# Two gate tiles to a bank, and the first chunk of the seven-product groups read at another distance

## The chip, the cores and the metric

One Trainium2 chip, one of its cores. The metric is the time of the whole launch in device microseconds (us), as the median of several runs.

## The reference

A two-layer decoder trunk in float32 on 256 tokens of width 2048. Layer 0 is a recurrent block (RG-LRU) and a SwiGLU feed-forward; layer 1 is sliding-window attention over one shared K/V and a second SwiGLU. What matters here:

```
def rg_lru(xb, w_rg, b_rg, w_ig, b_ig, lam):
    r = sigmoid(block_diag_linear(xb, w_rg, b_rg))      # 8 blocks of 256 x 256
    i = sigmoid(block_diag_linear(xb, w_ig, b_ig))
    log_a = -LRU_C * r * softplus(-lam)
    a = exp(log_a)
    u = sqrt(-expm1(2.0 * log_a)) * (i * xb)
    ...                                                 # h = scan of a*h + u
def recurrent_block(...):
    y_branch, x_branch = split(rms_norm(x, g) @ w_in)
    hs = rg_lru(conv(x_branch), ...)
    return x + (hs * gelu(y_branch)) @ w_out
def swiglu_ffn(x, g, w_in, w_out):
    gate, up = split(rms_norm(x, g) @ w_in)
    return x + (silu(gate) * up) @ w_out
```

## The kernel before

**Tiles and chunks.** Activations lie transposed, 128 features by 256 tokens to a tile. Each weight matrix is streamed once, in chunks of 128 x 1024 (512 KB: two blocks of 128 input features by 512 outputs). A chunk is a "job": `load` starts its DMA four jobs ahead into one of four `raw` buffers, `split` cuts it three jobs ahead into `hi` (ACT, L374) and `lo = raw - hi` (DVE, L375), one of four `hi` and four `lo` buffers, and the job's matmuls read them. A product of two float32 numbers is three matmuls, hi*hi, hi*lo and lo*hi. So an ordinary chunk is 24 matmuls of 128 x 128 by 256 columns (L422), and PE frees a `hi` buffer when the last matmul that reads it is done.

**The recurrent block.** `ORDER` sets the jobs: x groups (8 chunks each, then convolution), gate jobs g0 to g7 (one chunk of 24 matmuls each, L969) and y groups (8 chunks, then GELU), in the order x0 x1 x2 g0 x3 g1 y0 g2 g3 y1 g4 g5 y2 g6 g7 y3, and after them the projection `lru_out`. A gate job makes four 128 x 256 results, two for r and two for i. Before, each has its own PSUM bank of 512 columns, half of it unused, and ACT reads each with a Sigmoid. After every second gate job the task `recur` is started: Exp and Tanh on ACT, then products on DVE, Sqrt on ACT, a product and a scan (L1013) on DVE. The y task ends in `split_act`: a Copy on ACT and a subtraction on DVE give the tile z that `lru_out` multiplies with.

**Activation tables.** Sigmoid, Sqrt, and the pair Exp/Tanh each need another table on ACT. Where two neighbours on ACT's queue need different ones, an ACT_TABLE_LOAD stands between them.

**Order.** The kernel is recorded as one program; background tasks (convolution, `recur`, GELU, norms) are stepped between matmuls. A scheduling framework then orders each engine's queue by its own estimates of when operands are ready and puts in the waits. Dependences on PSUM go by whole banks. PSUM has eight banks; `bank()` hands out the one that has been free longest, `bank4()` a set of four.

**The seven-product groups.** In the input projection of each feed-forward, 9 of the 22 groups are `fast_group`s (`FAST`): in seven of their eight chunks (`PAIRS`; chunk 3 is plain) a 2 x 2 block product is done with seven products of 3 matmuls, 21 in place of 24 (L631). Three products read the chunk's `hi`/`lo`, four read mixed weights mh and ml that `mix` makes on DVE and ACT three jobs ahead. These are tiles of the pool `s0` to `s36`. A tile spacer of 64 bytes lies between `s0`-`s6` (the near ones) and `s7`-`s36` (the far ones); the mixed inputs lie in far tiles. "Distance" in this text is how far apart the two SBUF operands of a matmul lie, in bytes modulo 512: with mixed weights in near tiles it is 448, with far ones 0. A job's third entry chooses: 1 takes near tiles, 2 far ones.

```
            todo = ((5, part(a, 0), old(1)), (3, part(b, 0), old(3)), (2, com(3), old(2)),
                    (7, com(0), new(0)), (6, com(2), new(1)), (4, com(1), new(2)), (1, part(b, 1), new(3)))
            if c in self.EVEN:
                todo = todo[3:] + todo[:3]
```

Before chunk 4 the previous product group's results are transposed on PE (`flush`, L827). Elsewhere `LEVEL` names jobs whose `lo` lies so that eight of their matmuls have distance 0.

Of the kernel before, what the change touches and what calls it, by code (L numbers as in the profile page):

```python
# [14 lines left out]
AF = mybir.ActivationFunctionType  # L15
ALU = mybir.AluOpType

P = 128
D = 2048
T = 256  # L20
# [28 lines left out]
class Trunk:  # L49
# [16 lines left out]
    PLAIN = 4  # L66
    FAST = tuple(range(4, 21, 2))
    PAIRS = (0, 1, 2, 4, 5, 6, 7)
    EVEN = (0, 4)
    OWED = 9000.0  # L70
    BUSY = 780.0
    WORK = 37
# [551 lines left out]
    def fast_group(self, src, xn, mx, g, done, final):  # L624

        nc = self.nc
        st = {"begun": set()}

        def put(h, x, w, n=1):
            b = h // 2  # L630
            nc.tensor.matmul(st["ps"][b][:, h % 2 * T:(h % 2 + n) * T], x, w, start=b not in st["begun"], stop=True,  # L631
                             skip_group_check=True)
            st["begun"].add(b)

        def plain(c, hi, lo):

            x2 = [self.need(xn[2 * c + kt]) for kt in range(2)]
            wide = []
            for kt in range(2):
                for i in range(2):  # L640
                    xh, xl = (x2[kt][:, q * T + i * P:q * T + i * P + P] for q in range(2))
                    for x, w in ((xh, hi), (xl, hi), (xh, lo)):
                        wide.append((2 - 2 * i, x, w[:, kt * 2 * T:kt * 2 * T + 2 * T]))
            todo = [(h + e, x, w[:, e * T:e * T + T]) for h, x, w in wide for e in range(2)]
            for k, t in enumerate(todo):
                if k == len(todo) // 2:
                    self.half_tick()
                put(*t)

        def fast(c, hi, lo):  # L650

            a, b = (self.need(xn[2 * c + kt]) for kt in range(2))
            m = self.need(mx[c])
            mh, ml = self.mixed.pop(self.at)
            part = lambda s, q: (s[:, q * P:q * P + P], s[:, T + q * P:T + q * P + P])
            com = lambda q: (m[:, q * P:q * P + P], m[:, 2 * T + q * P:2 * T + q * P + P])
            old = lambda q: (hi[:, q * T:q * T + T], lo[:, q * T:q * T + T])
            new = lambda q: (mh[:, q * T:q * T + T], ml[:, q * T:q * T + T])
# [4 lines that stand above are left out]
            for n, (h, (xh, xl), (wh, wl)) in enumerate(todo):  # L663
                if n == 4:
                    self.half_tick()
                put(h, xh, wh)
                put(h, xl, wh)
                put(h, xh, wl)
            self.free(mh)
            self.free(ml)  # L670
            if final:
                self.free(m)

        for c in range(8):
            def mm(hi, lo, c=c):
                if c == 0:
                    st["ps"] = self.bank4()
                if c == self.EVEN[1]:
                    self.flush()
                (fast if c in self.PAIRS else plain)(c, hi, lo)  # L680
                if c == 7:
                    done(st["ps"])
            self.jobs.append((src(c), mm, (c in self.PAIRS) + (c in self.EVEN)))

# [225 lines left out]
    def lru(self, gains, rn):  # L910
        self.late = []
        nc, par = self.nc, self.par
# [45 lines left out]
        def gates(n):  # L958

            def mm(hi, lo):  # L960
                x2 = [self.need(xb[2 * n + kt]) for kt in range(2)]
                ps = [self.bank() for _ in range(4)]
                for j in range(4):
                    if j == 2:
                        self.half_tick()
                    for kt in range(2):
                        c = ((j // 2) * 2 + kt) * 256 + (j % 2) * P
                        for high, q in ((1, 0), (1, T), (0, 0)):
                            nc.tensor.matmul(ps[j][:, 0:T], (hi if high else lo)[:, c:c + P], x2[kt][:, q:q + T],  # L969
                                             start=kt == 0 and high > q, stop=kt == 1 and not high)  # L970
                v = []
                for j in range(4):
                    o = self.slot(F32)
                    col = (C_BR, C_BI)[j // 2] + 2 * n + j % 2
                    self.a(o[:, 0:T], ps[j][:, 0:T], AF.Sigmoid, bias=par[:, col:col + 1])
                    self.free_bank(ps[j])
                    v.append(o)
                for kt in range(2):
                    self.free(x2[kt])
                both.extend([(2 * n, v[0], v[2]), (2 * n + 1, v[1], v[3])])  # L980
                if n % 2:
                    self.spawn(recur(list(both)))
                    both.clear()
            self.jobs.append((self.d["gate"][n], mm, False))
# [3 lines left out]
        def recur(v):  # L988

            A = lambda s: s[:, 0:T]  # L990
            B = lambda s: s[:, T:2 * T]
            for k, r, i in v:
                self.a(B(r), A(r), AF.Exp, scale=self.cc[:, k:k + 1])
                self.a(A(r), A(r), AF.Tanh, scale=self.cc[:, 16 + k:17 + k])
                yield
                self.tt(B(i), A(i), A(xf[k]), ALU.mult)
                yield
            for k, r, i in v:
                self.stt(A(r), B(r), 1.0, A(r), ALU.add, ALU.mult)
                yield  # L1000
            for k, r, i in v:
                self.a(B(r), A(r), AF.Identity, bias=1.0)
                self.stt(A(r), A(r), 2.0, A(r), ALU.add, ALU.mult)
                yield
            for k, r, i in v:
                self.a(A(r), A(r), AF.Sqrt, scale=-1.0)
            yield
            for k, r, i in v:
                self.tt(A(i), A(r), B(i), ALU.mult)
                yield  # L1010
                self.dve += 350
                h = xf[k]
                self.nc.vector.tensor_tensor_scan(A(h), B(r), A(i), 0.0, ALU.mult, ALU.add)  # L1013
                hs[k].ap = h
                hs[k].ready = True
                self.free(r)
                self.free(i)
                yield
# [465 lines left out]
```

## Time and profile before

| | |
|---|---|
| median of 3 runs | 1943.24 us (1942.21 to 1943.66) |
| the profiled execution | 1942.83 us |
| its span, first to last instruction | 1941.0 us |
| PE / DVE / ACT busy | 1935.5 / 1521.2 / 1118.3 us |
| granted clock of PE over the span | 1.000 |

The recurrent block with its projection takes the first 320 us or so, the first feed-forward runs to about 1020 us, K/V and attention to 1190 us, and the second feed-forward takes the rest. Times in the rows are us from the span's start. A matmul's own duration is longer than its place in the stream: matmuls overlap, so what one costs is the time from its start to the next one's.

### The profile page before, as it was taken

To read this page: it belongs to the slowest core of one execution; us is meant where nothing else is said; L and a number is where in the kernel's file an instruction comes from. 1 tells how busy PE (TensorE), PEld (TensorE's weight loads), DVE (VectorE), ACT (ScalarE), POOL (GpSimd) and SP (SyncE) were. 2 spreads that over 40 slices of the span, in tenths; PEclk is the share of its full clock that TensorE was granted. 3 is DMA by queue.
4 is the path that set the end of the run, shared out by engine and by line. 5 is a ranking of instruction groups with operands and counts; after the bars stand their busy time and mean duration, and the time that the engine had idled before them with its cause. 6 is when DMAs were issued, how large, how long until landed. Compare 5 with 4: busy or idle time off the path is not lost.

```text
span 1941.0 us, 40252 instructions
## 1 busy us (share of the span) xinstructions
PE 1935.5 (100%) x16604; PEld 1908.5 (98%) x16604; DVE 1521.2 (78%) x2356; ACT 1118.3 (58%) x1583; POOL 4.4 (0%) x12
## 2 busy tenths in 40 slices
PE   9999999999999999999999999999999999999999
PEld 9999999999999999999998789999999999999999
DVE  7989868999989988545667886799999989944443
ACT  7798746556555557434556765555555555743332
POOL 0000000000000000000000000000000000000000
PEclk9999999999999999999999999999999999999999
DMA  8555666566665557565555435665656666666663
GB/s 282 185 184 186 218 217 196 188 206 208 206 204 199 193 200 255 187 198 193 195 186 193 144 120 198 204 199 193 206 199 205 211 206 202 237 198 206 206 202 125
DMA packets 107576, 385.36 MB, mean 199 GB/s; under 512 B 12032, under 2 KB 14208, under 8 KB 107392
## 3 DMA queue, kind: packets, MB, share of 16 engines
q1 hardware_dynamic: 106848, 381.86, 59.2%
q8 instruction: 130, 2.13, 0.4%
q0 software_dynamic: 256, 0.52, 0.1%
q14 instruction: 54, 0.44, 0.1%
q10 hardware_dynamic: 288, 0.40, 0.1%
HBM read 375.92 MB, written 6.29 MB: 197 GB/s over the span
## 4 chain that ended last, share of the span: by engine, by line
PE 97%; DVE 1%; ACT 1%; issue 0%; DVEq 0%; ACTq 0%
PE b L422 68%; PE b L631 18%; PE b L1369 5%; PE b L603 2%; PE b L1206 1%; DVE lo L375 1%; PE b L1163 1%; ACT s L137 1%; PE b L827 0%; DVE s L150 0%; PE b L1282 0%; PE b L1255 0%; ACT hi L374 0%; ACT L137 0%; PE b L1413 0%
## 5 line engine op out<-in xcount | busy, mean ns | idle before, releaser
L422 PE MATMUL b<-s,hi 128*128 128x256 f32 x7936 | 1018.6, 276 | 0.8 <-ACT s L137 0.7
L422 PEld LDWEIGHTS b<-s,hi 128*128 128x128 f32 x7936 | 962.1, 188 | 1.8 <-ACT s L137 1.2
L375 DVE TENSOR_TENSOR lo<-raw,hi 128x1024 fp32r<-128x1024 f32 (+1 forms) x579 | 702.0, 1219 | 332.5 <-ACT hi L374 323.6
L374 ACT ACTIVATE hi<-raw 128x1024 fp32r<-128x1024 f32 (+1 forms) x579 | 607.7, 1056 | 483.0 <-PE b L422 416.2
L422 PE MATMUL b<-s,lo 128*128 128x256 f32 x3968 | 586.2, 277 | 0.0
L422 PEld LDWEIGHTS b<-s,lo 128*128 128x128 f32 x3968 | 512.8, 188 | 0.0
L389 ACT ACTIVATE s<-s 128x1024 fp32r<-128x1024 f32 x126 | 131.6, 1057 | 169.6 <-DVE s L388 169.6
L631 PE MATMUL b<-s,s 128*128 128x256 f32 x1512 | 195.9, 279 | 0.0
L631 PEld LDWEIGHTS b<-s,s 128*128 128x128 f32 x1512 | 183.0, 189 | 0.0
L631 PE MATMUL b<-hi,s 128*128 128x256 f32 x1044 | 178.0, 277 | 0.0
L391 DVE TENSOR_TENSOR s<-s,s 128x1024 fp32r<-128x1024 f32 x126 | 153.5, 1219 | 5.9 <-ACT s L389 5.9
L631 PEld LDWEIGHTS b<-hi,s 128*128 128x128 f32 x1044 | 152.4, 188 | 0.0
L631 PE MATMUL b<-lo,s 128*128 128x256 f32 x522 | 132.5, 276 | 0.0
L390 DVE TENSOR_TENSOR lo<-raw,hi 128x768 fp32r<-128x768 f32 x126 | 118.4, 950 | 0.0
L137 ACT ACTIVATE s<-s 128x512 fp32r<-128x512 f32 (+3 forms) x179 | 87.7, 521 | 52.5 <-DVE s L146 31.1
L386 DVE TENSOR_TENSOR s<-raw 128x512 f32<-128x512 f32 x126 | 86.4, 686 | 39.4 <-DMA raw<-in_ffn_in 39.1
L385 ACT ACTIVATE hi<-raw 128x768 fp32r<-128x768 f32 x126 | 102.8, 834 | 12.3 <-ACT s L389 6.4
L631 PEld LDWEIGHTS b<-lo,s 128*128 128x128 f32 x522 | 92.7, 188 | 0.0
L1369 PE MATMUL b<-hi,s 128*128 128x512 f32 x256 | 81.5, 400 | 0.0
L146 DVE TENSOR_TENSOR s<-s,s 128x512 fp32r<-128x512 f32 (+2 forms) x145 | 75.8, 549 | 2.0 <-ACT s L137 2.0
L137 ACT ACTIVATE s<-s,par 128x256 fp32r<-128x256 f32 (+1 forms) x96 | 46.6, 513 | 26.0 <-DVE s L146 25.3
L146 DVE TENSOR_TENSOR s<-b,s 128x512 f32<-128x512 f32 (+2 forms) x106 | 55.5, 554 | 3.8 <-ACT s L137 2.5
(119 smaller groups left out, 1132.4 us busy)
## 6 DMA issues: line engine op xcount, KB each, us to landing
raw<-in_ffn_in SPq DMA_DIRECT2D x352, 512.0 KB, 3.4
raw<-in_ffn_out SPq DMA_DIRECT2D x176, 512.0 KB, 4.2
raw<-in_lru_in SPq DMA_DIRECT2D x63, 512.0 KB, 4.0
raw<-in_lru_out SPq DMA_DIRECT2D x32, 512.0 KB, 3.5
raw<-in_w_q SPq DMA_DIRECT2D x32, 512.0 KB, 3.3
raw<-in_w_o SPq DMA_DIRECT2D x32, 512.0 KB, 3.3
raw<-in_gate SPq DMA_DIRECT2D x8, 512.0 KB, 3.9
away<-s SPq DMA_DIRECT2D x8, 512.0 KB, 3.8
```

Of the source, the lines that this page charges most:

```text
L137: self.nc.scalar.activation(out, in_, func, **kw)
L146: self.nc.vector.tensor_tensor(out, a, b, op)
L374: self.nc.scalar.activation(hi[:, q], raw[:, q], AF.Copy)
L375: self.nc.vector.tensor_tensor(lo[:, q], raw[:, q], hi[:, q].bitcast(F32), ALU.subtract)
L385: act(hi[:, q], raw[:, q], AF.Copy)
L386: tt(two(d[:, 0:2 * T]), two(raw[:, T:3 * T]), raw[:, 0:T].unsqueeze(1).to_broadcast([P, 2, T]), ALU.subtract)
L389: act(mh[:, :], d[:, :], AF.Copy)
L390: tt(lo[:, q], raw[:, q], hi[:, q].bitcast(F32), ALU.subtract)
L391: self.mark = tt(ml[:, :], d[:, :], mh[:, :].bitcast(F32), ALU.subtract)
L422: self.nc.tensor.matmul(ps[f][:, 0:c1 - c0], w, x2[k][:, c0:c1], start=f not in begun, stop=last and all(q[1] != f for q in todo[n + 1:]))
L631: nc.tensor.matmul(st["ps"][b][:, h % 2 * T:(h % 2 + n) * T], x, w, start=b not in st["begun"], stop=True, skip_group_check=True)
L1369: nc.tensor.matmul(st[g][b][:, :], x, q, start=c + kt == 0 and x is xh and q is wh, stop=c == 7 and kt == 1 and q is wl)
```

## The change

A gate job takes two banks in place of four and writes two results to each. The accumulation is opened by the first matmul of the bank alone, and a bank is given back after its second Sigmoid. In the product groups `EVEN` keeps chunk 4 alone: chunk 0 now takes near tiles for its mixed weights and does its `hi`/`lo` products first, as chunks 1, 2, 5, 6 and 7 do. The place of the transposes (`TURN`) stays before chunk 4.

```diff
-    EVEN = (0, 4)
+    EVEN = (4,)
+    TURN = 4
...
-                if c == self.EVEN[1]:
+                if c == self.TURN:
                     self.flush()
                 (fast if c in self.PAIRS else plain)(c, hi, lo)
...
             def mm(hi, lo):
                 x2 = [self.need(xb[2 * n + kt]) for kt in range(2)]
-                ps = [self.bank() for _ in range(4)]
+                ps = [self.bank() for _ in range(2)]
+                cut = [ps[j // 2][:, j % 2 * T:j % 2 * T + T] for j in range(4)]
                 for j in range(4):
                     if j == 2:
                         self.half_tick()
                     for kt in range(2):
                         c = ((j // 2) * 2 + kt) * 256 + (j % 2) * P
                         for high, q in ((1, 0), (1, T), (0, 0)):
-                            nc.tensor.matmul(ps[j][:, 0:T], (hi if high else lo)[:, c:c + P], x2[kt][:, q:q + T],
-                                             start=kt == 0 and high > q, stop=kt == 1 and not high)
+                            nc.tensor.matmul(cut[j], (hi if high else lo)[:, c:c + P], x2[kt][:, q:q + T],
+                                             start=j % 2 + kt == 0 and high > q, stop=True, skip_group_check=True)
...
-                    self.a(o[:, 0:T], ps[j][:, 0:T], AF.Sigmoid, bias=par[:, col:col + 1])
-                    self.free_bank(ps[j])
+                    self.a(o[:, 0:T], cut[j], AF.Sigmoid, bias=par[:, col:col + 1])
+                    if j % 2:
+                        self.free_bank(ps[j // 2])
```

The change moves instructions on every engine of the recurrent block, since other banks and other times of readiness go into the framework's order. In the whole program ACT has 25 table loads before and 31 now; the six more all stand between g3 and the end of y3. The first place is ACT's queue at the gate jobs g2 and g3. Tiles `s_1679` and `s_1682` are g2's, `s_1714` and `s_1717` g3's; `<-b` rows are Sigmoids, `cc` rows Exp and Tanh, and `hi_80`, `hi_81`, `hi_78` splits of later chunks. Before, from the first Sigmoid of g3 on:

```order
L137 ACTIVATE s_1714<-b_143,par 128x256
L137 ACTIVATE s_1714<-b_144,par 128x256
L137 ACTIVATE s_1717<-b_145,par 128x256
L137 ACTIVATE s_1717<-b_142,par 128x256
L137 ACT_TABLE_LOAD
L137 ACTIVATE s_1679<-s_1679,cc 128x256 x4
L374 ACTIVATE hi_81<-raw_77 128x1024
L137 ACTIVATE s_1714<-s_1714,cc 128x256 x4
L374 ACTIVATE hi_78<-raw_74 128x1024
```

The same place now:

```order
L138 ACTIVATE s_1714<-b_145,par 128x256 x2
L138 ACT_TABLE_LOAD
L138 ACTIVATE s_1679<-s_1679,cc 128x256
L138 ACT_TABLE_LOAD
L138 ACTIVATE s_1717<-b_142,par 128x256 x2
L138 ACTIVATE s_1679<-s_1679,cc 128x256
L138 ACT_TABLE_LOAD
L138 ACTIVATE s_1679<-s_1679,cc 128x256
L375 ACTIVATE hi_81<-raw_77 128x1024
L138 ACTIVATE s_1679<-s_1679,cc 128x256
L138 ACTIVATE s_1714<-s_1714,cc 128x256 x4
L375 ACTIVATE hi_78<-raw_74 128x1024
```

Two Sigmoids of g3 have moved behind an Exp, so there are two more table loads ahead of the split of `hi_81`, and one Exp or Tanh fewer. At g4 and g5, and again at g6 and g7, a Sqrt task is cut in the same way, with two more loads each. The second place is ACT's queue after y3 has left PE. Tiles `s_2371` and `s_2414` carry the Sqrt of g6 and g7, `s_2692`, `s_2883` and `s_2886` the Tanh of y3, and `s_2898` is the z tile of `lru_out`'s seventh chunk. Before:

```order
L137 ACT_TABLE_LOAD
L137 ACTIVATE s_2371<-s_2371 128x256
L374 ACTIVATE hi_80<-raw_76 128x1024
L137 ACTIVATE s_2371<-s_2371 128x256
L137 ACTIVATE s_2414<-s_2414 128x256 x2
L137 ACTIVATE s_2692<-h_90 128x256
L137 ACTIVATE s_2883<-h_91 128x256
L374 ACTIVATE hi_81<-raw_77 128x1024
L137 ACTIVATE s_2883<-h_92 128x256
L137 ACTIVATE s_2886<-s_2692 128x256
L374 ACTIVATE hi_78<-raw_74 128x1024
L137 ACT_TABLE_LOAD
```

Now, from the split that comes next after that of `hi_78`:

```order
L375 ACTIVATE hi_79<-raw_75 128x1024
L138 ACT_TABLE_LOAD
L138 ACTIVATE s_2371<-s_2371 128x256 x2
L138 ACTIVATE s_2414<-s_2414 128x256 x2
L375 ACTIVATE hi_80<-raw_76 128x1024
L375 ACTIVATE hi_81<-raw_77 128x1024
L375 ACTIVATE hi_78<-raw_74 128x1024
L138 ACT_TABLE_LOAD
L138 ACTIVATE s_2692<-s_2692 128x256
L138 ACTIVATE s_2883<-s_2883 128x256
L375 ACTIVATE hi_79<-raw_75 128x1024
```

The Sqrt stood ahead of the splits of the second half of `lru_out`'s first group; now it stands behind four more splits (those of `hi_80`, `hi_81`, `hi_78`, `hi_79`), and the Tanh behind a further three. On PE, 11 matmuls of the next group now stand ahead of the first that reads `s_2898`. The third place is PE's queue at chunk 0 of a product group, with `s9_5114` and `s16_5115` the mixed weights and `s15_3902` and `s27_3922` the inputs. Before:

```order
L631 MATMUL b3_144<-s9_5114,s27_3922 128x256 x2
L631 MATMUL b3_144<-s16_5115,s27_3922 128x256
...
L631 MATMUL b0_141<-s9_5114,s15_3902 128x256 x2
L631 MATMUL b0_141<-s16_5115,s15_3902 128x256
L631 MATMUL b2_143<-hi0_78,s15_3902 128x256 x2
L631 MATMUL b2_143<-lo0_82,s15_3902 128x256
```

Now:

```order
L632 MATMUL b2_143<-hi0_78,s15_3902 128x256 x2
L632 MATMUL b2_143<-lo0_82,s15_3902 128x256
...
L632 MATMUL b3_144<-s0_5114,s27_3922 128x256 x2
L632 MATMUL b3_144<-s5_5115,s27_3922 128x256
L632 MATMUL b3_144<-s0_5114,s27_3922 128x256 x2
L632 MATMUL b3_144<-s5_5115,s27_3922 128x256
```

The nine matmuls on `hi` and `lo` come first, and the twelve on mixed weights read `s0` and `s5`, near tiles, where they read `s9` and `s16`, far ones. So it is in all 18 product groups.

## Rows read from the trace of the kernel before

**Rows 1.** The page: span, and busy time of each engine.

```profile
span 1941.0 us, 40252 instructions
PE 1935.5 (100%) x16604; PEld 1908.5 (98%) x16604; DVE 1521.2 (78%) x2356; ACT 1118.3 (58%) x1583; POOL 4.4 (0%) x12
```

**Rows 2.** Two stretches: length, busy us of each engine, clock, DMA share, GB/s.

```profile
127.00:227.00 100.00, 99.03 (x858) 98.06 (x857) 89.92 (x168) 88.43 (x163) 0.00 (x0) 1.00 0.57 185
382.00:753.00 371.00, 371.00 (x3262) 371.00 (x3261) 339.71 (x471) 218.67 (x264) 0.00 (x0) 1.00 0.61 207
```

**Rows 3.** Timeline of PE where y2 begins: start, us, what, count.

```profile
155.28 0.28 PE L969 MATMUL b<-s,lo 128*128 128x256 f32 x1
155.69 1.59 PE L422 MATMUL b<-s,hi 128*128 128x256 f32 x8
157.11 1.12 PE L422 MATMUL b<-s,lo 128*128 128x256 f32 x8
```

**Rows 4.** Timeline of PE at g7 and where y3 begins.

```profile
180.68 0.28 PE L969 MATMUL b<-s,lo 128*128 128x256 f32 x1
181.11 0.48 PE L969 MATMUL b<-s,hi 128*128 128x256 f32 x2 [0.15 <-DVE h L146]
...
183.90 0.28 PE L969 MATMUL b<-s,lo 128*128 128x256 f32 x1
184.87 1.59 PE L422 MATMUL b<-s,hi 128*128 128x256 f32 x8 [0.69 <-ACT s L137]
```

**Rows 5.** The critical chain in `w_o`: start, us, what; the same matmuls twice.

```profile
1133.34 8.18 PE b L603 x72
...
1166.29 8.48 PE b L603 x72
```

**Rows 6.** Timeline of PE at a product group's chunks 0 and 1.

```profile
423.75 1.60 PE L631 MATMUL b<-s,s 128*128 128x256 f32 x12
...
426.22 0.39 PE L631 MATMUL b<-hi,s 128*128 128x256 f32 x2
...
427.24 1.52 PE L631 MATMUL b<-s,s 128*128 128x256 f32 x12
428.60 0.39 PE L631 MATMUL b<-hi,s 128*128 128x256 f32 x2
```

**Rows 7.** Timeline of ACT after the Sigmoids of g3.

```profile
130.80 1.28 ACT L137 ACT_TABLE_LOAD   x1
132.09 1.71 ACT L137 ACTIVATE s<-s,cc 128x256 f32<-128x256 f32 x4
133.71 1.05 ACT L374 ACTIVATE hi<-raw 128x1024 fp32r<-128x1024 f32 x1
```

**Rows 8.** Timeline of ACT: splits of later chunks of y1's and y3's surroundings.

```profile
165.15 1.05 ACT L374 ACTIVATE hi<-raw 128x1024 fp32r<-128x1024 f32 x1
...
188.15 1.10 ACT L374 ACTIVATE hi<-raw 128x1024 fp32r<-128x1024 f32 x1
```

**Rows 9.** Timeline of PE: the first matmuls that read three splits.

```profile
136.35 1.41 PE L422 MATMUL b<-s,hi 128*128 128x256 f32 x11
...
169.91 0.84 PE L422 MATMUL b<-s,hi 128*128 128x256 f32 x6
...
193.65 1.07 PE L422 MATMUL b<-s,hi 128*128 128x256 f32 x8
```

**Rows 10.** Timeline of PE in `lru_out`: chunks two and seven of its first group.

```profile
211.84 1.86 PE L422 MATMUL b<-s,hi 128*128 128x256 f32 x15
...
223.68 1.98 PE L422 MATMUL b<-s,hi 128*128 128x256 f32 x16
```

**Rows 11.** Timeline of DVE after y3: a scan, a split, two elementwise steps.

```profile
215.20 0.68 DVE L1013 TENSOR_TENSOR_SCAN s<-s,s 128x256 f32<-128x256 f32 x1
...
218.46 1.22 DVE L375 TENSOR_TENSOR lo<-raw,hi 128x1024 fp32r<-128x1024 f32 x1
219.60 0.75 DVE L146 TENSOR_TENSOR s<-s,s 128x256 fp32r<-128x256 f32 x2
```

## The prediction

> **What bounds the kernel now.** I read the page first [rows 1]: PE is busy for 1935.5 of a span of 1941.0 us at the full granted clock, DVE for 1521.2, ACT for 1118.3. So an edit pays only through PE's stream: by a shorter step from one matmul's start to the next, or by a wait that goes or comes. Then the two stretches that the change touches [rows 2]. Where the product groups are, 382 to 753 us, PE is busy for all of 371.00 us and ACT for only 218.67. In the recurrent block, 127 to 227 us, PE is busy for 99.03 of 100.00 and ACT for 88.43: ACT has 11.6 us to spare there, and less than that in any one place. The little idle time of PE is read in its timeline around the gates [rows 3, 4].
>
> Two more readings carry sizes. The first is what a wait leaves behind. In the projection after attention the same 72 matmuls take 8.18 us, and 8.48 us after a wait [rows 5]: 0.1136 and 0.1178 us each. The slow step of 0.0042 us per matmul more stays until a chunk comes in which eight matmuls have distance 0; how many matmuls lie between is counted in the program. The second is distance: of two neighbouring product chunks with the same 21 matmuls, chunk 0 (mixed weights at distance 0) takes 426.22 - 423.75 = 2.47 us and chunk 1 (at 448) 428.60 - 426.22 = 2.38 [rows 6].
>
> **The product groups.** Nothing is added or removed there: twelve matmuls of chunk 0 go from distance 0 to 448, and nine on the chunk's own weights go first. Chunk 0 becomes a chunk 1: 0.09 us less, in 18 groups: 18 x 0.09 = 1.6 us. The near tiles are shared with the chunks before and after, so the mixing for chunk 1 may have to wait a little longer for them; ACT's 152 us to spare in 371 [rows 2] cover that, and chunks 1, 2 and 5 to 7 already follow each other so without a wait. From below: no gain, if the step depends on something else than distance; from above 2 us. I take -1.6.
>
> Beside this stands a rule of the Trainium skill (SBUF — State Buffer, section on who interferes with whom): PE reads moving data and weights through two independent ports and waits for nobody there. By it distance could not matter and this term would be 0. The rows say otherwise: the twelve mixed matmuls alone are busy for 1.60 us in chunk 0 and 1.52 in chunk 1 [rows 6]. The row decides.
>
> **Waits for banks that go.** With four banks to a gate job, what comes after the gates finds banks that ACT has just read. Three such waits are in the trace. At y2's start: 155.69 - 155.28 = 0.41 between starts where 0.11 is the step, so 0.30, and then eight matmuls that take 1.42 in place of 8 x 0.113 = 0.91, which is 0.51 [rows 3]: 0.81. In g7: 0.43 - 0.11 = 0.32, a late first matmul of about 0.09, and 24 at the slow step (0.1): 0.5. At y3's start: 0.97 - 0.11 = 0.86, and the eight slow ones again, since the row has the same 1.59 for them (0.51): 1.37 [rows 4]. With two banks to a job y2 and y3 get banks that were freed several chunks earlier. Sum: -2.7.
>
> **Six table loads that come.** The price of the smaller tiles is on ACT's queue. Two Sigmoids share a bank, dependence goes by banks, and so the first Sigmoid of a bank now waits for all twelve of its matmuls in place of six. The framework sees them ready later and puts an Exp, or a Sqrt, between them: six loads more. A load is 1.28 us and the next instruction starts 1.29 after it [rows 7]; with the overlap that two neighbours otherwise have (four Exp/Tanh take 1.62, so 0.40 each; a duration is longer than its step by 0.1) one costs ACT's queue 1.40. Six are 8.4 us, against 11.6 idle. What reaches PE is a matter of place: ACT's splits are what PE waits for.
>
> A, at g2 and g3. Two loads more and one Exp fewer ahead of the split of `hi_81`: 2 x 1.40 - 0.40 = 2.4 us. The split now ends at 133.71 + 1.05 = 134.76 [rows 7], PE reads it at 136.35 [rows 9]. 1.6 us of cover; 0.8 is left as a wait. The first matmul after it costs 0.1, and 168 matmuls come before the next eight at distance 0: 168 x 0.0042 = 0.7. A: 1.6 us.
>
> B, at g4 and g5. The split ends at 165.15 + 1.05 = 166.20 [rows 8], PE reads it at 169.91 [rows 9]: 3.7 us of cover. ACT enters late by A's 1.6, has two loads (2.8) and one step of Sqrt and one of Sigmoid more ahead of the split (0.7): 5.1. Less 3.7, and less the 0.8 by which PE itself is still late there (A's 1.6, with y2's 0.8 given back), leaves 0.6; with 0.1 and 129 x 0.0042 = 0.5, B: 1.2 us.
>
> C, at g6 and g7. The split ends at 189.25 [rows 8], PE reads it at 193.65 [rows 9]: 4.4 of cover. ACT enters 2.0 late (as PE is before g7: 1.6 + 1.2 - 0.8), has two loads (2.8) and three Sqrt (0.9) more ahead: 5.7. Less 4.4 and a PE that is then 0.1 late (2.8 less the 2.7 of the waits gone) leaves 1.2; with 0.1 and 153 x 0.0042 = 0.6, C: 1.9 us.
>
> D, after y3. The Sqrt of g6 and g7 stood ahead of the splits of `lru_out`; now it stands behind the split of `hi_79`, whose buffer PE frees at about 211.84 + 7 x 0.113 + 0.28 = 212.9 [rows 10], and PE is 2.0 late by then: 214.9. Split 1.05, load 1.3 and two Sqrt 0.7: DVE can take up the rest at some 218 to 219. It owes four products at 0.34, four scans at 0.6, three `lo` splits at 1.14 and eight elementwise steps at 0.34 (0.75 for two that overlap [rows 11]): 1.4 + 2.4 + 3.4 + 2.7 = 9.9 us, and ACT's Copy 0.4 on top. PE wants z at 223.68 [rows 10] + 2.0 + 11 x 0.113 = 226.9, since eleven matmuls now stand ahead. 218.5 + 9.9 + 0.4 = 228.8 to 229.9 for 219.6: late by 1.9 to 3.0. I take 2.2, as ACT and DVE share waits that I count twice. z comes in halves, and the second stands behind a `lo` split (1.22 [rows 11]): another 0.65, and 0.45 for three late first matmuls, a last small wait and the slow step. D: 3.3 us.
>
> If ACT's idle time hid all of it, A to D would be 0; if no cover helped, six loads are 8.4 and D's 3.3 come on top: 11.7. A trace with such loads in these places isn't there. I take 1.6 + 1.2 + 1.9 + 3.3 = 8.0.
>
> Against this stands another rule of the skill (ScalarE: Activation LUTs, section on what ACT_TABLE_LOAD costs): a switch is about 1.28 us for the load and about 1.38 for the drain around it. The load agrees; of a drain nothing is seen in the row, where the next Exp starts 1.29 after the load. By the page six loads would be an estimated 16 us of ACT, more than it has idle. The same page's section on table sets says to batch by set, which this order undoes.
>
> **Sum.** -1.6 - 2.7 + 8.0 = +3.7 us. The profiled execution took 1942.83 (span 1941.0 and 1.83 around it), the median is 0.41 higher: 1946.5 by the one and 1946.9 by the other. I say 1946.6.
>
> **Rivals.**
> 1. Not slower: ACT swallows the loads. For it: 11.6 us idle against 8.4, and splits done 1.6 to 4.4 us early [rows 7 to 9]. Then only the first two terms stand: -4.3, 1938.8. It decides by one number: how late the split of `hi_81` ends. If it ends before 136.35, nothing starts to slip. Against it: 2.4 of work in 1.6 of cover.
> 2. The three splits are late, but y3's z comes in time, because DVE takes the products and scans earlier than I let it, ahead of `lo` splits. Then D is 0: 4.7 - 4.3 = +0.4, 1943.5. For it: D's 9.9 us are a sum of many small steps, and 3 of them are enough. Against it: the Sqrt's place on the queue is fixed, behind a split that PE releases.
> 3. More: a late split also makes the `hi` buffers and loads behind it late, so one wait becomes two or three in the chunks that follow, and each sets the slow step anew. At A to C another 0.1 + 0.7 each and a second wait of 0.5 at one or two, D at its far end (+0.8): about +4, 1950.5.
> 4. A table switch stops ACT for twice the load's time, where its queue is full. Two loads in place are then 2 x 1.3 more late at A, B and C, of which the later lose what PE is already late: some 2.6 + 2 x 1.3 = 5 more, 1952. No drain shows in [rows 7], so little speaks for it. It is the skill's figure, taken as a mechanism.
> 5. Distance does nothing for chunk 0: +5.3, 1948.4. Rows 6 speak against it.
>
> **How the numbers follow.** The forecast has a chance of 0.50 (its own range 1944.8 to 1948.6), rival 1 0.08, rival 2 0.19, rival 3 0.15, rival 4 0.03, rival 5 0.05. Changes within 0.2%, that is 3.9 us, can't be told from none here. The forecast lies just inside: I put 0.28 of its 0.50 within and 0.22 slower. Same: 0.28 + 0.19 + 0.01 of rival 5 = 0.48; slower: 0.22 + 0.15 + 0.03 + 0.04 = 0.44; faster: rival 1, 0.08. The range from 1942.6 to 1950.2 leaves out rival 1, some of rival 3 and rival 4.
>
> **What the profile would show.** Right: 31 loads on ACT; chunk 0 at 2.38; no gap on PE where y2, y3 and g7 begin; PE waits for ACT near 137, 171 and 195, of 0.8, 0.6 and 1.2 us, each with a slow step behind it; and a wait of some 2 us for z near 227. PE late against before by about 2 us as y3 ends and by 5 after `lru_out`'s first group, then less by 1.6 over the product groups. Wrong: no wait at 137 (rival 1), no wait at 227 (rival 2), or a chunk 0 still at 2.47 (rival 5).

## The result, and the profile after

The changed kernel takes 1957.61 us (median of 6 runs, 1955.85 to 1959.25), the one before 1942.97: 1.0075 times as long, 95% interval 1.0062 to 1.0088. Forecast were 1946.6 us and a range up to 1950.2. The direction was right, the size was not: 14.6 us lost, not 3.7. The profiled execution of the changed kernel took 1959.25 us, the slowest of its six; its span is 16.5 us longer than that of before, so the trace shows about 2 us more of a loss than the medians do.

To see where, take the start of the n-th matmul in a trace less the start of the n-th in the trace of before. "After" is the changed kernel; the other columns are experiments (below). Places are times of the kernel before; the first column's differences of up to 1 us arise in the first 20 us and are not the change's.

| us later at | 127 | 154 | 212 | 280 | 376 | 804 | 1693 | 1793 |
|---|---|---|---|---|---|---|---|---|
| after | 0.2 | 2.0 | 3.4 | 8.4 | 8.4 | 11.0 | 13.8 | 16.4 |
| gates alone (e1) | -0.8 | 1.1 | 1.4 | 7.3 | 7.3 | 7.3 | 7.5 | 7.5 |
| distance alone (e2) | -0.1 | -0.1 | -0.1 | -0.1 | -0.1 | 2.6 | 5.5 | 8.1 |
| gates, Sqrt held (e5) | -0.2 | -0.2 | -2.9 | -2.9 | -3.0 | -3.0 | -2.6 | -2.6 |
| two loads added (e6) | -0.4 | 0.8 | 0.7 | 6.2 | 6.2 | 6.2 | 6.6 | 6.6 |
| both mended (e8) | 0.2 | 0.2 | -2.5 | -2.5 | -2.6 | -2.9 | -2.9 | -2.9 |

Half of the loss (8.2 us) stands in the recurrent block and `lru_out`, half (8.0 us) where a gain of 1.6 was forecast: 2.6 in each feed-forward's product groups, 2.7 in one stretch behind the last of them, and 0.1 between.

The page of the changed kernel, and two stretches (columns as in [rows 1, 2]):

```profile
span 1957.5 us, 40297 instructions
PE 1948.0 (100%) x16604; PEld 1920.7 (98%) x16604; DVE 1523.3 (78%) x2356; ACT 1133.2 (58%) x1589; POOL 4.4 (0%) x12
```

```profile
127.00:227.00 100.00, 97.64 (x829) 96.78 (x828) 83.35 (x152) 92.39 (x161) 0.00 (x0) 1.00 0.55 179
382.00:753.00 371.00, 371.00 (x3239) 371.00 (x3238) 339.43 (x470) 219.24 (x259) 0.00 (x0) 1.00 0.61 203
```

In the recurrent block PE now has 2.4 us without work where it had 1.0, and ACT 4 us more to do. In the product groups PE is as busy as before, every microsecond of 371, and yet does 3239 matmuls where it did 3262. Nothing waits there: each matmul takes a longer step.

**The product groups.** The chain of waits gives the 87 matmuls of a group's chunks 0 to 3 as one piece (start, us, what). Before, then after:

```profile
423.91 9.96 PE b L631 x87
```

```profile
432.60 10.25 PE b L632 x87
```

That is +0.29 a group. The timeline of PE there shows what runs, and where it ends:

```profile
432.09 0.39 PE L423 MATMUL b<-s,hi 128*128 128x256 f32 x2
432.32 0.28 PE L423 MATMUL b<-s,lo 128*128 128x256 f32 x1
432.43 0.40 PE L632 MATMUL b<-hi,s 128*128 128x256 f32 x2
432.67 0.28 PE L632 MATMUL b<-lo,s 128*128 128x256 f32 x1
...
433.50 1.58 PE L632 MATMUL b<-s,s 128*128 128x256 f32 x12
434.91 0.40 PE L632 MATMUL b<-hi,s 128*128 128x256 f32 x2
```

Three matmuls took 432.43 - 432.09 = 0.34 us in the ordinary chunk, and the group's first nine take 433.50 - 432.43 = 1.07, 0.36 for three, with no gap ahead of them. The twelve mixed ones are now at distance 448 and step by (434.91 - 433.50) / 12 = 0.1175, not by the 0.1133 of a chunk 1 before [rows 6]. The mean of the 87 is 0.1178: the same slow step as behind a wait in [rows 5]. It ends at chunk 4, whose twelve are at distance 0.

**The stretch behind the last group.** The last transposes stand in the second ordinary group behind the product groups. Before, 522 matmuls run in the 58.90 us from then on, at 0.113; in the changed kernel 503 in 59.00, at 0.117 (columns as in [rows 2]):

```profile
1702.80:1761.70 58.90, 58.90 (x522) 58.90 (x521) 28.17 (x27) 23.36 (x22) 0.00 (x0) 1.00 0.62 201
```

```profile
1717.00:1776.00 59.00, 59.00 (x503) 59.00 (x502) 26.74 (x26) 22.26 (x21) 0.00 (x0) 1.00 0.58 188
```

The clock is 1.00 in both. The slow step lasts past one block of eight at distance 0 (at 1715.95), in the trace of e2 as well, and ends at the next one.

**The gates.** The waits for banks of [rows 3, 4] are gone. PE where y2 begins, and where y3 begins:

```profile
157.35 0.28 PE L971 MATMUL b<-s,lo 128*128 128x256 f32 x1
157.47 1.10 PE L423 MATMUL b<-s,hi 128*128 128x256 f32 x8
158.41 0.76 PE L423 MATMUL b<-s,lo 128*128 128x256 f32 x5
...
186.92 0.28 PE L971 MATMUL b<-s,lo 128*128 128x256 f32 x1
187.04 0.63 PE L423 MATMUL b<-s,hi 128*128 128x256 f32 x4
```

Steps of 0.12 ahead of both, and eight matmuls in 0.94, not 1.42. In their place stand waits for splits. ACT's timeline at g2 and g3:

```profile
130.28 1.28 ACT L138 ACT_TABLE_LOAD   x1
131.57 0.51 ACT L138 ACTIVATE s<-s,cc 128x256 f32<-128x256 f32 x1
132.10 1.28 ACT L138 ACT_TABLE_LOAD   x1
133.39 0.84 ACT L138 ACTIVATE s<-b,par 128x256 f32<-128x256 f32 x2
134.12 0.51 ACT L138 ACTIVATE s<-s,cc 128x256 f32<-128x256 f32 x1
134.65 1.28 ACT L138 ACT_TABLE_LOAD   x1
135.94 0.51 ACT L138 ACTIVATE s<-s,cc 128x256 f32<-128x256 f32 x1
136.36 1.04 ACT L375 ACTIVATE hi<-raw 128x1024 fp32r<-128x1024 f32 x1
```

The split that stood at 133.71 [rows 7] now stands at 136.36. (The Tanh at 134.12 follows two Sigmoids with no load between: not every change between Sigmoid and the pair Exp/Tanh costs a load, as "Activation tables" above has it.) The matmuls of [rows 9] wait for this split and for its two likes; the place at 166.28 is a fourth, which was not forecast. PE's timeline there:

```profile
135.67 1.07 PE L423 MATMUL b<-s,lo 128*128 128x256 f32 x8
137.45 2.15 PE L423 MATMUL b<-s,hi 128*128 128x256 f32 x16 [0.71 <-ACT hi L375]
...
166.28 1.45 PE L423 MATMUL b<-s,hi 128*128 128x256 f32 x10 [0.36 <-ACT hi L375]
...
172.80 1.45 PE L423 MATMUL b<-s,hi 128*128 128x256 f32 x10 [0.59 <-ACT hi L375]
...
196.27 1.92 PE L423 MATMUL b<-s,hi 128*128 128x256 f32 x14 [0.70 <-ACT hi L375]
```

A wait in this text is a start less the start before it, less one step: here 137.45 - 135.67 - 8 x 0.113 = 0.87. The idle time in brackets is smaller, since a matmul's own duration is longer than its step. The four waits are 0.87, 0.52, 0.76 and 0.87.

Then z. PE's timeline in `lru_out`, and the stretches around it (the clock is the third number from the end):

```profile
227.15 1.41 PE L423 MATMUL b<-s,hi 128*128 128x256 f32 x11
230.61 0.85 PE L423 MATMUL b<-s,hi 128*128 128x256 f32 x5 [2.05 <-ACT s L138]
231.97 2.18 PE L423 MATMUL b<-s,hi 128*128 128x256 f32 x12 [0.50 <-DVE s L147]
233.95 1.91 PE L423 MATMUL b<-s,lo 128*128 128x256 f32 x8
```

```profile
228.40:230.50 2.10, 0.16 (x2) 0.00 (x0) 2.10 (x6) 1.27 (x5) 0.00 (x0) 1.00 0.64 209
230.50:233.20 2.70, 2.08 (x14) 1.88 (x15) 2.70 (x7) 0.39 (x2) 0.00 (x0) 0.94 0.59 202
233.20:236.30 3.10, 3.10 (x17) 3.10 (x16) 1.16 (x4) 1.78 (x3) 0.00 (x0) 0.50 0.35 130
236.30:240.00 3.70, 3.70 (x33) 3.70 (x33) 2.94 (x7) 1.26 (x2) 0.00 (x0) 1.00 0.41 142
```

Eleven matmuls, a wait of 2.2 us for the first half of z, five more, a wait of 0.7 for the second: as walked. But then the granted clock falls to 0.50, the level of 1.2 GHz, for 3.4 us (all of the third stretch and, by its mean of 0.94, 0.3 us of the second): fifteen matmuls step by 0.213 in place of 0.113, which is 1.5 us.

### The profile page after: what moved, and what is told of

Its sections match the earlier page's. It is cut to its first block, busy times and chain, and to the rows that moved or that the text cites. A ratio compares the mean times of both kernels' runs of the same rounds, so it can differ in the third digit from the quotient of the medians.

```text
span 1957.5 us, 40297 instructions
## 1 busy us (share of the span) xinstructions
PE 1948.0 (100%) x16604; PEld 1920.7 (98%) x16604; DVE 1523.3 (78%) x2356; ACT 1133.2 (58%) x1589; POOL 4.4 (0%) x12
## 4 chain that ended last, share of the span: by engine, by line
PE 96%; ACT 2%; DVE 1%; issue 1%; DMA 0%; ACTq 0%; DVEq 0%
PE b L423 66%; PE b L632 18%; PE b L1372 5%; PE b L604 2%; ACT s L138 1%; ACT L138 1%; PE b L1209 1%; ACT hi L375 1%; DVE lo L376 1%; PE b L1166 1%; DVE s L151 0%; PE b L828 0%; PE b L1285 0%; PE b L1258 0%; PE b L1416 0%
```

## The experiments

**e1: the gates alone.** Against the changed kernel:

```diff
-    EVEN = (4,)
+    EVEN = (0, 4)
```

> The gates in two banks alone; EVEN stays (0, 4), so chunk 0 keeps its far tiles and its old order. Theory S (the changed kernel's loss has two separate parts: 8.4 us from the gates up to 240 us, and 0.28 us in each of the 18 product groups, because a slow step of 0.118 us in place of 0.1136 begins where a group begins and the distance-0 matmuls of chunk 0 were what ended it): the same 31 table loads and waits as after, +8.4 us by 240 us, nothing in the groups; 1951 to 1952, ratio 1.0043. Rival B (the groups are slow only because the gates' waits left PE or the far tiles in another state): the groups are slow here too, near 1956. My prediction's own sum without the distance term would be +5.3, 1948.3.

Measured: 1949.77 us, ratio 1.0035 (1.0023 to 1.0048), +6.7. The trace has the table loads and waits of the changed kernel, and the product groups are fast again; the chain's piece:

```profile
431.18 9.96 PE b L632 x87
```

So the gates alone do not slow the groups; with e2, where the distance alone does, rival B falls.

**e2: the distance alone.** Against the kernel before:

```diff
-    EVEN = (0, 4)
+    EVEN = (4,)
+    TURN = 4
```

> The distance change alone (EVEN = (4,), chunk 0 near and its hi/lo products first); gates in four banks. Theory S: chunks 0 to 3 of each product group run at 0.118 us per matmul, +0.28 us in each of 18 groups, +5 us: 1948, ratio 1.0026. Rival B: the groups are fast without the gates' change, -1.6 us: 1941.4, ratio 0.9992 (my prediction's term).

Measured: 1950.49 us, ratio 1.0038 (1.0026 to 1.0051), +7.5. Nothing differs up to 376 us; then 2.6 us are lost in each feed-forward, as theory S has it, and 2.7 more behind the last group, which it did not name. e1 and e2 together lose 14.2 us, the changed kernel 14.6: two separate parts.

**e3: chunk 0's order alone.** Hi/lo products first, the mixed ones still at distance 0:

```diff
-            if c in self.EVEN:
+            if c == 4:
                 todo = todo[3:] + todo[:3]
```

> Only the order of chunk 0's products is changed: hi/lo products first, the mixed ones still on far tiles at distance 0. Theory S: the slow step lasts for the nine first matmuls only and the twelve at distance 0 end it: 9 x 0.0042 = 0.04 us per group, +0.7 us in all, 1943.7, chunks 1 to 3 at 0.1136. Rival A (not the distance but the new order, hi/lo products first, starts the slow step): it lasts to chunk 4 as in the changed kernel, +5 to +6 us, 1948 to 1949.

Measured: 1944.05 us, ratio 1.0004 (0.9995 to 1.0013), +1.0, within the interval of no change and of the 0.7 expected. The piece of 87, and PE's timeline of chunk 0 and of chunk 1's mixed ones:

```profile
424.21 9.99 PE b L631 x87
```

```profile
424.05 0.40 PE L631 MATMUL b<-hi,s 128*128 128x256 f32 x2
...
425.11 1.59 PE L631 MATMUL b<-s,s 128*128 128x256 f32 x12
426.54 0.40 PE L631 MATMUL b<-hi,s 128*128 128x256 f32 x2
...
427.58 1.52 PE L631 MATMUL b<-s,s 128*128 128x256 f32 x12
```

The nine first ones take 1.06 us, 0.118 each, with no mixed tile read yet: the slow step begins where the group begins, whatever tiles it uses. Behind the twelve at distance 0 chunk 1 is fast (1.52). Rival A falls: not the order, the distance-0 matmuls decide how long it lasts.

**e4: three at distance 0.** The distance alone, and chunk 0's `lo` 64 bytes further (`lev0` holds the first jobs of the product groups):

```diff
-        return (q[i % 4][:, a:a + 1024] for q, a in ((self.hi, o), (self.lo, self.LEVEL.get(i, o))))
+        return (q[i % 4][:, a:a + 1024] for q, a in ((self.hi, o), (self.lo, self.LEVEL.get(i, 16 if i in self.lev0 else o))))
```

> As the distance change alone, but chunk 0's lo lies 64 bytes further, so that its three lo matmuls (not neighbours: each stands behind two on hi) are at distance 0. Theory S1 (any distance-0 matmul ends the slow step): nine fewer at 0.0067 more, less a few slow ones at the group's start: about -0.05 us a group, -0.9 us, 1942.0. Theory S2 (a row of them is needed): the slow step lasts to chunk 4, +5.2 us, 1948.2.

Measured: 1942.55 us, ratio 0.9996 (0.9987 to 1.0005), -0.5. The piece is shorter than before:

```profile
422.99 9.93 PE b L633 x87
```

Three such matmuls do what twelve did, and the stretch behind the last group is fast too. Against e2 the edit is worth 7.9 us: this is the run that shows what ends the slow step, and with it the cause of the groups' loss. That it beats the kernel before is within the interval.

**e5: the gates, with Sqrt held in place.** Gates in two banks, EVEN as before, and each Sqrt pinned behind what was recorded ahead of it on ACT (`ka` is `a` with that pin):

```diff
-                self.a(A(r), A(r), AF.Sqrt, scale=-1.0)
+                self.ka(A(r), A(r), AF.Sqrt, scale=-1.0)
```

> The gates in two banks as in the changed kernel, chunk 0 as before, and one edit more: each Sqrt of the recurrent block is pinned on ACT's queue behind what was recorded before it. The queue then has 23 table loads where the gates alone have 31 and the kernel before 25, and no Sigmoid or Sqrt task is cut. Theory L (the gates' loss is the loads and the late Sqrt on ACT's queue, not the half banks): the PE waits near 137, 172, 195 and 228 us go, the waits for banks at y2, g7 and y3 stay away: -2.7 us against before, 1940.3, ratio 0.9986. Rival H (half-used against full banks cost by themselves, PE writing a bank while ACT reads its other half): the loss of the gates alone stays, about +6.7, 1949.7.

Measured: 1940.19 us, ratio 0.9986 (0.9977 to 0.9995), -2.6. The recurrent block (columns as in [rows 2]), then ACT at g3:

```profile
127.00:227.00 100.00, 100.00 (x881) 100.00 (x880) 91.88 (x174) 88.09 (x162) 0.00 (x0) 1.00 0.59 189
```

```profile
129.88 1.28 ACT L138 ACT_TABLE_LOAD   x1
131.17 1.71 ACT L138 ACTIVATE s<-s,cc 128x256 f32<-128x256 f32 x4
132.78 1.05 ACT L379 ACTIVATE hi<-raw 128x1024 fp32r<-128x1024 f32 x1
```

ACT has 23 table loads. PE has no idle time there, and the clock stays at 1.00. The half banks cost nothing; the price was the order on ACT's queue. What is left is the second term of the prediction's sum: -2.7 forecast, -2.7 in the table from 127 to 280 us. By matmul starts it comes in three steps, 0.81 us where y2 begins, 0.47 in g7 and 1.41 where y3 begins; the walk had 0.81, 0.5 and 1.37. The pin with four banks to a job was not run.

**e6: two loads added.** The kernel before, at g3's Exp:

```diff
             for k, r, i in v:
+                if k == 4:
+                    for q in ("sqrt_and_others", "sigmoid_and_others"):
+                        self.tc.keep_in_program_order(self.nc.scalar.preload_act_table_set(q))
                 self.a(B(r), A(r), AF.Exp, scale=self.cc[:, k:k + 1])
```

> The kernel before, four banks to a gate job, with two table loads that do nothing put on ACT's queue behind the Sigmoids of g3, where the changed kernel has its two (29 loads in all, as the order after this place changes too). It measures what two loads cost at A. Theory L, by the prediction's walk: 2 x 1.29 = 2.6 us on ACT, 1.6 of it covered, so PE waits 1.0 us for the split of hi_81 near 136, 0.1 for the first matmul and 0.7 at the slow step: 1.8 us later than before by 155 us; the end between 1944.8 and 1950, by what the later loads do. If a load cost twice its time (the rival with a drain): the wait is 3.6 us. If ACT's idle time covers it: no wait.

Measured: 1950.06 us, ratio 1.0037 (1.0024 to 1.0049), +7.3. ACT, and PE at the split's first reader:

```profile
130.46 2.57 ACT L995 ACT_TABLE_LOAD   x2
133.04 1.28 ACT L137 ACT_TABLE_LOAD   x1
134.33 1.71 ACT L137 ACTIVATE s<-s,cc 128x256 f32<-128x256 f32 x4
135.95 1.04 ACT L374 ACTIVATE hi<-raw 128x1024 fp32r<-128x1024 f32 x1
```

```profile
135.09 1.07 PE L422 MATMUL b<-s,lo 128*128 128x256 f32 x8
137.04 2.08 PE L422 MATMUL b<-s,hi 128*128 128x256 f32 x16 [0.88 <-ACT hi L374]
```

Three loads in a row take 134.33 - 130.46 = 3.87 us, 1.29 each, and PE waits 137.04 - 135.09 - 8 x 0.113 = 1.04: the walk of A to a tenth. The Trainium skill (ScalarE: Activation LUTs, section on what ACT_TABLE_LOAD costs) has some 1.28 us for the load, which agrees, and a drain about as long on top, which these rows do not show. PE is 1.2 us late behind it and still 1.2 late at 155 us, where 1.8 was expected: no slow step followed this wait, so the 0.7 for it was not sure. The rest of the +7.3 comes from the order behind this place, which changed too: a wait of 1.77 in g7, and waits of 1.89 and 1.58 for z with the clock at 0.80 and 0.76 over the stretches 225 to 230 and 230 to 233 us.

**e7: two banks for g4 to g7 alone.** Against e1, `w` being the results in one bank:

```diff
-                ps = [self.bank() for _ in range(2)]
-                cut = [ps[j // 2][:, j % 2 * T:j % 2 * T + T] for j in range(4)]
+                w = 2 if n>3 else 1
+                ps = [self.bank() for _ in range(4 // w)]
+                cut = [ps[j // w][:, j % w * T:j % w * T + T] for j in range(4)]
...
```

> Two banks for the gate jobs g4 to g7 alone, four for g0 to g3; chunk 0 as before. ACT's queue has 25 table loads, as before. Theory L: no wait for a split near 137, 172 or 195, none for z near 228, and the waits for banks where g7, y2 and y3 begin are gone: -2.7 us, 1940.3. Rival H: half of the gates' loss stays, +3 us or more.

Measured: 1941.10 us, ratio 0.9993 (0.9984 to 1.0001), -1.7, with no change still inside the interval. The order has 25 loads, no wait for a split; by 212 us it is 2.7 us ahead, then it loses 1.2 of that in `lru_out`, with PE busy throughout:

```profile
210.00:233.00 23.00, 22.99 (x194) 22.69 (x194) 21.95 (x42) 17.62 (x30) 0.00 (x0) 1.00 0.65 224
```

Behind a wait of 0.04 us at 212.4 the step is 0.118 up to 231 us, and a few more waits of under 0.2 us come on top. Why they come here was not followed up. Rival H falls here too.

**e8: both parts, both mended.** The changed kernel with the `lo` of e4 and the pin of e5.

> Both parts of the change, each with what its loss is put down to taken away: the Sqrt pinned as in the run with the gates alone, and chunk 0 near with three lo matmuls at distance 0. By theories S1 and L the two gains add: -2.7 and -0.5 as measured for the three: -3.2 us, 1939.8, ratio 0.9984. If the two parts of the loss are tied to each other, it is slower than before.

Measured: 1939.51 us, ratio 0.9984 (0.9975 to 0.9993): 3.3 us less than the 1942.80 of the kernel before, where -3.2 was expected, and 18.1 less than the changed kernel. The two parts do not hinder each other. It beats both kernels; over e5 alone its 0.7 us are no more than the interval, so that the second gain adds to the first is not shown by the times.

## Why the prediction was wrong

**The step that failed: "Chunk 0 becomes a chunk 1: 0.09 us less, in 18 groups".** Its sign was wrong: +0.29 a group, 5.2 us, and 2.7 behind the last one, in place of -1.6. [rows 6] was read rightly, but chunk 0 did not become a chunk 1: it takes 434.91 - 432.43 = 2.48 us now, where it took 2.47, and the loss is in the chunks behind it. Chunk 0 and chunk 1 had stood in different states. The slow step begins at a group's first matmul, with no wait (e3), and in the kernel before chunk 0's own block at distance 0 had ended it before chunk 1 was measured. The 0.09 us that chunk 0 cost more bought the fast step for the 75 matmuls behind its twelve. The prediction had this rule at hand, from [rows 5] and the program, and used it only behind waits. The 5.2 is (10.25 - 9.96) x 18. None of the five rivals held it; rival 5 (distance does nothing) was nearest in kind, with the term at 0.

**Waits for banks that go: right.** -2.7, by e5 to a tenth.

**Six table loads: right in place, short in size.** A to C were walked to 4.7 us and are 4.8 in e1 (2.1 us late from 127 to 212, with the 2.7 of e5 given back). A's wait was put at 0.8 and is 0.87; B's 0.6 is 0.76 in the changed kernel and 0.53 in e1; C's 1.2 is 0.87. In the changed kernel A to C cost 5.9: one wait more, at 166.28, for a split that ACT reached late. The likely reason is an earlier split on its queue, at 151.19, that waited 1.93 us for its raw chunk to land (0.94 in e1); no run varied that. That is the mechanism of rival 3, in a small way.

**D: mis-sized by the clock.** 3.3 forecast, 5.0 measured (8.4 - 3.4 between 212 and 280 us; 5.9 in e1, where the slow step went on behind 240 us). The waits fit: 2.2 and 0.65 forecast, 2.21 and 0.67 measured. That the 2.2 fits so well is partly luck: it was picked from 1.9 to 3.0, for a PE 2.0 us late, and PE was 3.2 late there. What was missing is the fall of the granted clock to 0.50 behind them, 15 x (0.213 - 0.113) = 1.5 us. It fell in e1 and e6 as well, each time behind two waits near each other (2.21 and 0.66, 1.89 and 1.58); behind A's single wait of 0.87, and behind a single one of 1.77 in e6's g7, it stayed at 1.00.

**ACT swallows the loads (rival 1):** fell. ACT had 7.6 us left idle from 127 to 227 us and PE still waited four times.

**Open.** Why the slow step begins at a group's start; why it came behind the last transposes in e2 and the changed kernel but not in e1, e4 and e8; why one block of eight did not end it at 1715.95; and why A's wait brought it in the changed kernel but not in e6. No run varied that alone.

## What to carry to other kernels

Before an expensive-looking pattern is replaced, look at what follows it: the cost of a chunk may be paid for its neighbours, and a comparison of two neighbours in one trace doesn't show that, since both ran with the pattern in place. Where buffers are merged, read the queue of the engine that empties them: a coarser dependence let the framework put other work between, and one pin on that queue turned +6.7 us into -2.6. A walk of a wait from cover and added work was good to 0.4 us a place here, though it missed one place; what came after the wait, the clock and the step, was not.

## What the runs showed of the hardware

- The same matmuls ran at two steps, 0.113 and 0.118 us, at a granted clock of 1.00 and with PE busy throughout; three matmuls at distance 0, none next to another, were enough to end the slower one in 18 places (e4), and a row of eight failed at one place, in the changed kernel and in e2.
- Waits of PE of 2.2 and 0.7 us within 4 us were followed by 3.4 us at the clock level of 1.2 GHz (e1 too); single waits of 0.87 and 1.77 us were not.
- Table loads in a row take 1.29 us each, and the instruction behind the last one starts at once.
